# The diagonals, the first queries' weights, the value scaling and the turned heads of a decoder block, placed anew

## The chip, the cores and the metric

The kernel runs on one core of one Trainium2 chip. The metric is the device time of one execution in microseconds (us). The kernel before took 1434.86 us, the median of 3 runs (1434.17 to 1435.17).

## What is computed

One layer of a decoder block on x of 1024 positions by 1024 channels, in float32. The input is normalized by rows and projected; two branches work on the projection, differential attention with a distance bias and chunkwise retention; sigmoid gates merge them; a gated MLP with a short causal convolution follows. Cut to what matters:

```python
h = rms_norm(x, g_mix)                       # 1024 x 1024
q1, q2, k1, k2, va, qr, kr, vr, gr, gate_a, gate_r = split(h @ w_in)
# differential attention: 4 heads, keys of 64, values of 128 channels
s1 = q1 @ k1.T / 8 - slope * dist            # causal; s2 from q2, k2 likewise
a = (softmax(s1) - lam * softmax(s2)) @ va
a = rms(a) * g_diff_sub * (1 - lam_init)     # by head
r = rms(retention(qr, kr, vr)) * silu(gr)    # 4 heads, chunks of 128
merged = sigmoid(gate_a) * (a @ w_diff_proj) + sigmoid(gate_r) * (r @ w_ret_proj)
x = x + merged @ w_out
zg, zu = split(causal_dwconv(rms_norm(x, g_ffn) @ w_up))
x = x + (silu(zg) * zu) @ w_down
out = rms_norm(x, g_final)
```

## The kernel before, in words

**Precision.** Every large product is made of three TensorE products of rounded float32 parts. An operand is split into a part "hi" (a copy of rounded type, made by ACT) and a part "lo" (what the copy lacks, a subtraction on DVE or POOL); then hi x hi, hi x lo and lo x hi go into one PSUM bank. `split`, `product` and `gemm` (L206, with `weight` at L163 and L164 for the weights) do that.

**The first stretch.** It is written in plain order and laid out by a scheduler that puts each instruction on its engine as soon as its inputs are due. x comes in eight blocks of 128 channels. The values of heads 0 and 1 (`ps_va0`) and 2 and 3 (`ps_va1`) are multiplied from x times the gain `g_mix`, before the rows' norms are known: `u` holds the split parts of that product, in pool places "br", "c", "vo" and "s". The norms of the rows stand in `rst_x` (two tiles of 128 x 4, one for each half of the positions). `to_va` (L395) copies a bank of values into `va[h]` on ACT; later POOL multiplies each `va[h]` by `rst_x` in two halves (L433), eight products in all. `across` (L262, L263) spreads `rst_x` along a row: DVE makes four diagonal tiles, one TensorE product with ones turns them into `row_x`, a bank of 128 x 512, for each half. x is loaded again as it was, eight blocks of 512 KB into six places "s", and normalized (L418 to L420): DVE multiplies by gain and row, ACT makes the hi part `hT[0]`, and the lo part `hT[1]` is made by DVE for the first half of the positions (c = 0) and by POOL for the second (c = 1).

**The attention.** `queries_keys(h)` multiplies the queries and the keys of a head from hT: a bank `psq` or `psk` for each half of the positions, 24 products of 128 x 512 in each. Its weights come through the pools "wraw", "whi" and "wlo" of two places each; POOL makes their lo parts. Both banks of a product come from the two banks of PSUM tag "g". ACT and DVE empty them (L471 on, L478 to L481). For each block of 128 queries `attention` multiplies scores `pss` (banks "x"), which DVE adds to the distance table `dist_t` while it takes the minimum (L507), ACT exponentiates them (L512), DVE joins the two maps, TensorE transposes the result (`pat`, banks "b", L525), ACT empties that (L527), TensorE multiplies by the values (`po`, L530). `dist_t` is the one tile of pool tag "g" from then on; `ssum` holds that place before it. Its load is issued on POOL's queue (L438). The products for the queries and keys of the second and of the third head run between the blocks of the first head's attention.

**The steps.** From the fourth head on the order is written by hand. A step is 24 products of 128 x 512 or some 12 of them (24 for two halves); `step` notes its loads, sums, products and what follows them (`post`), and `issue` puts out the loads 9 steps ahead, sums 4, hi parts 3 and lo parts 2 steps ahead, then what stands in `pre` of the step, then its products, then its `post`. `at_step` appends to the `post` of a step; `n_gates` is the number of the first step of the attention's output projection (`ps_pa`). The last seven steps before it are parts of the gates' products, named (pair, part): (11,2), (10,4), (11,5), (11,6), (11,3), (11,7), (11,4). `turn_a(h)` (L787) transposes head h's attention output, eight 128 x 128 transposes into the two banks "b"; `finish_a(h)` empties these banks, first two ACT copies to the hi part (L803), then two DVE subtractions to the lo part (L805). Both stand in a post:

```python
at_step(n_gates - 7 + h, partial(turn_a, h))
at_step(n_gates - 6 + h, partial(finish_a, h))
```

so head h+1's transposes come behind the products of step n_gates - 6 + h, and head h's emptying behind those same products' own emptying.

## Time and profile before

| | |
|---|---|
| runs, us | 1434.86 median of 3 (1434.17 to 1435.17) |
| the profiled execution, us | 1434.84, of which its span 1433.0 |
| mean clock granted to TensorE | 0.984 |
| TensorE (PE) busy | 1368.6 us, 96%, 6472 instructions |
| VectorE (DVE) busy | 1068.0 us, 75%, 1699 instructions |
| ScalarE (ACT) busy | 703.4 us, 49%, 1318 instructions |
| GpSimd (POOL) busy | 154.3 us, 11%, 92 instructions |
| HBM traffic | 136.81 MB read, 49.55 MB written |

Busy time is the time in which an engine has an instruction at work, from one profiled execution. All durations quoted further on are of that execution; its 1434.84 us are the span and 1.84 us around it. [...]

### The profile page before, as it was taken

The page shows a single profiled execution, that of the slowest core. Times are in us where ns is not written, and L with a number is a line of the kernel's source. Part 1 is how long each engine was busy: PE and PEld are TensorE (multiplying, and loading weights), DVE is VectorE, ACT ScalarE, POOL GpSimd, SP SyncE. Part 2 cuts the span into 40 slices and gives each one's busy share as a digit, 9 for nine tenths or more (in the row PEclk, how much of TensorE's full clock was granted, in tenths as well). Part 3 has the DMA queues.
Part 4 walks back from the last instruction along what each step waited for, and adds up shares of the span by engine and source line. Part 5 has one row for each costly group of instructions (what it writes and reads, how often), then busy time and mean ns, then how long its engine had stood idle before and what let it go on. Part 6 is the DMA issues. An engine that isn't in the chain of part 4 may idle for free.

```text
span 1433.0 us, 18055 instructions
## 1 busy us (share of the span) xinstructions
PE 1368.6 (96%) x6472; PEld 1134.0 (79%) x6472; DVE 1068.0 (75%) x1699; ACT 703.4 (49%) x1318; POOL 154.3 (11%) x92
## 2 busy tenths in 40 slices
PE   7899899989999998999998989999999999999996
PEld 7887788878888886788776767888888888888885
DVE  6759765675655553467968989888988899897876
ACT  6544665564454434221445465455555556444452
POOL 6711001000000000000000012111111112200000
PEclk9999999999999999999989999999999999999997
DMA  7313101314334332635324134434433365943223
GB/s 250 125 45 121 56 16 45 137 70 143 137 125 136 108 110 81 251 138 180 153 100 148 59 113 159 133 122 136 139 126 125 125 228 195 331 165 103 94 90 118
DMA packets 81018, 187.55 MB, mean 131 GB/s; under 512 B 8320, under 2 KB 18944, under 8 KB 80928
## 3 DMA queue, kind: packets, MB, share of 16 engines
q1 hardware_dynamic: 80736, 185.74, 37.8%
q8 instruction: 51, 0.84, 0.2%
q0 software_dynamic: 192, 0.66, 0.1%
q14 instruction: 39, 0.32, 0.1%
HBM read 136.81 MB, written 49.55 MB: 130 GB/s over the span
## 4 chain that ended last, share of the span: by engine, by line
PE 42%; DVE 7%; ACT 1%; issue 1%; DVEq 0%; ACTq 0%
PE up L276 24%; PE wd L276 14%; PE wo L276 4%; DVE wf L285 1%; DVE f L285 1%; DVE x L1461 1%; DVE y L1381 1%; DVE ssum L228 1%; DVE x L1230 1%; DVE x L288 1%; DVE x L285 0%; ACT f L291 0%; DVE zg L288 0%; DVE raw_zg L285 0%; DVE wwo L285 0%
## 5 line engine op out<-in xcount | busy, mean ns | idle before, releaser
L276 PE MATMUL up<-f,wf 128*128 128x512 f32 x1848 | 424.8, 391 | 9.2 <-DVE wf L285 3.4
L276 PEld LDWEIGHTS up<-f,wf 128*128 128x128 f32 x1848 | 345.3, 188 | 88.1 <-DVE wf L285 6.4
L276 PE MATMUL wd<-awd,wwd 128*128 128x512 f32 (+1 forms) x960 | 212.2, 383 | 0.0
L276 PEld LDWEIGHTS wd<-awd,wwd 128*128 128x128 f32 x960 | 176.0, 189 | 35.4 <-issue 0.5
L285 POOL TENSOR_TENSOR t12g<-y 128x512 f32<-128x512 f32 x11 | 19.8, 1796 | 673.3 <-DVE y L1391 538.4
L276 PE MATMUL wo<-awo,wwo 128*128 128x512 f32 x336 | 83.2, 407 | 7.4 <-DVE awo L285 7.1
L276 PEld LDWEIGHTS wo<-awo,wwo 128*128 128x128 f32 x336 | 64.9, 196 | 24.8 <-DVE awo L285 10.1
L512 ACT ACTIVATE s<-s,row 128x512 f32<-128x512 f32 (+7 forms) x64 | 49.5, 773 | 26.7 <-DVE row L507 26.2
L1381 DVE SCALAR_TENSOR_TENSOR y<-zg,par,y 128x1022 f32<-128x1022 f32 (+1 forms) x44 | 58.6, 1333 | 2.9 <-ACT y L1378 2.9
L502 PE MATMUL pss<-k,q 128*128 128x512 f32 (+2 forms) x192 | 52.8, 371 | 5.6 <-DVE row L507 5.5
L288 DVE TENSOR_TENSOR zg<-zg,up 128x512 f32<-128x512 f32 x44 | 30.2, 685 | 37.0 <-PE up L276 34.6
L1381 DVE SCALAR_TENSOR_TENSOR y<-zu,par,y 128x1022 f32<-128x1022 f32 (+1 forms) x44 | 56.1, 1277 | 0.0
L291 ACT ACTIVATE zg<-up 128x512 f32<-128x512 f32 x44 | 26.1, 596 | 58.5 <-PE up L276 58.5
L285 DVE TENSOR_TENSOR awd<-act_in,awd 128x512 fp32r<-128x512 f32 x77 | 53.7, 697 | 0.0
L507 DVE CUSTOM_DVE_ANT_0 s<-pss,dist_t 128x512 f32<-128x512 f32 (+3 forms) x64 | 37.0, 587 | 21.1 <-PE pss L502 19.7
L291 ACT ACTIVATE awd<-act_in 128x512 fp32r<-128x512 f32 x77 | 47.5, 616 | 0.3 <-DVE wf L285 0.2
L276 PE MATMUL ps_pa<-a,wpa 128*128 128x512 f32 x192 | 46.0, 394 | 0.0
L206 PE MATMUL psq<-hT,hi_q 128*128 128x512 f32 x128 | 43.2, 415 | 2.5 <-ACT hi_q L163 1.7
L291 ACT ACTIVATE zu<-up 128x512 f32<-128x512 f32 x44 | 26.2, 596 | 39.2 <-PE up L276 39.1
L276 PE MATMUL ps_pr<-r,wpr 128*128 128x512 f32 x192 | 43.7, 389 | 0.0
L291 ACT ACTIVATE wwd<-wdv 128x512 fp32r<-128x512 f32 x33 | 20.9, 632 | 46.1 <-PE wd L276 37.1
L530 PEld LDWEIGHTS po<-va,at 128*128 128x128 f32 x288 | 38.1, 195 | 6.2 <-ACT at L527 4.1
(367 smaller groups left out, 2822.9 us busy)
## 6 DMA issues: line engine op xcount, KB each, us to landing
act_in<-act SPq DMA_DIRECT2D x77, 256.0 KB, 2.9
act<-y SPq DMA_DIRECT2D x55, 256.0 KB, 2.2
raw_zg<-in_wall SPq DMA_DIRECT2D x22, 512.0 KB, 3.4
raw_zu<-in_wall SPq DMA_DIRECT2D x22, 512.0 KB, 4.1
x<-in_x SPq DMA_DIRECT2D x15, 512.0 KB, 7.8
act<-t12g SPq DMA_DIRECT2D x22, 256.0 KB, 2.0
wdu<-in_wall SPq DMA_DIRECT2D x22, 256.0 KB, 4.8
wdv<-in_wall SPq DMA_DIRECT2D x22, 256.0 KB, 5.7
```

What stands on the lines that cost most here:

```text
L206: nc.tensor.matmul(ps, w, a, start=i == 0, stop=i == n - 1)
L228: engine.tensor_tensor(self.ssum, self.ssum, sq, op=ALU.add)
L276: nc.tensor.matmul(ps[:, cols], w[:, x * 512 + at : x * 512 + at + P], a[y][:, cols], start=start and i == 0, stop=stop and i == n - 1, sk ...
L285: engine.tensor_tensor(out, a, b, op=ALU.subtract)
L288: engine.tensor_tensor(out, a, b, op=ALU.add)
L291: nc.scalar.activation(out, a, AF.Copy)
L502: nc.tensor.matmul(ps[:, : max(n, 256)], qs[m][:, i * P : (i + 1) * P], k[:, c : c + max(n, 256)], start=e == 0, stop=e == 1,)
L507: nc.vector.tensor_tensor_reduce(s[:, c : c + n], ps[:, :n], dst_t[:, S - width + c : S - width + c + n], SLOPES[h], low_, op0=ALU.add, op ...
L512: nc.scalar.activation(s[:, :width], s[:, :width], AF.Exp, bias=low_, scale=-1.0, accum_out=z[:, m : m + 1])
L530: nc.tensor.matmul(po, at[:, k * P : (k + 1) * P], va[h][:, kb, :], start=kb == 0, stop=kb == i)
L1230: nc.vector.scalar_tensor_tensor(y, y, gain(1, at), row, op0=ALU.mult, op1=ALU.mult)
L1381: nc.vector.scalar_tensor_tensor(y[side][:, n:], z[:, : S - n], t[:, j : j + 1], y[side][:, n:], op0=ALU.mult, op1=ALU.add)
```

## The change

It has five parts.

1. `across`: the eight diagonal tiles `diag_x` are made by ACT (a copy scaled by a column of `rst_x`) instead of DVE.
2. The values of heads 2 and 3 are multiplied by `rst_x` where ACT empties their banks. POOL's four products for these two heads are gone; the four for heads 0 and 1 stand behind the first head's queries and keys in the program text.
3. x is loaded again by halves of its rows: eight pieces of 256 KB for the first 512 positions, then eight for the second, two to a place of pool "s". DVE makes the lo part for both halves.
4. The first head's query weights have places of their own: the hi part in a place "br" (`q_br`), the lo part in the place "g" that `ssum` leaves and `dist_t` takes (`q_g`). Their load and split stand ahead of the normalizing, and DVE makes their lo part and that of the first key weights. The first head's products go queries c = 0, keys c = 0, queries c = 1, keys c = 1, with banks of "g" and "x" in turn.
5. `finish_a(h)` stands in the `pre` of step n_gates - 6 + h, ahead of its products, instead of in its `post`.

```diff
--- before.py
+++ after.py
@@ -259,7 +259,7 @@
         n = r.shape[1]
         diag = t4("at", f"diag_{name}", shape=(P, 512))
         for i in range(n):
-            nc.vector.tensor_scalar(diag[:, i * P : (i + 1) * P], ident, r[:, i : i + 1], None, op0=ALU.mult)
+            nc.scalar.activation(diag[:, i * P : (i + 1) * P], ident, AF.Copy, scale=r[:, i : i + 1])
         nc.tensor.matmul(ps, ones, diag[:, : n * P], start=True, stop=True)
         return ps
 
@@ -390,9 +390,9 @@
             if k == 3:
                 nc.sync.dma_start(out=cst, in_=consts)
 
-        def to_va(st, p, ps):
+        def to_va(st, p, ps, scale=1.0):
             for h in range(2 * p, 2 * p + 2):
-                nc.scalar.activation(va[h][:, st, :], ps[:, h % 2 * DV : (h % 2 + 1) * DV], AF.Copy)
+                nc.scalar.activation(va[h][:, st, :], ps[:, h % 2 * DV : (h % 2 + 1) * DV], AF.Copy, scale=scale)
 
         for st in range(NST):
             to_va(st, 0, first_ps[st])
@@ -411,26 +411,18 @@
                     for k in range(KB)
                 ],
             )
-            to_va(st, 1, ps)
-
-        def normalize(src, h, k, cs, g, row, dst, helper):
-
-            nc.vector.scalar_tensor_tensor(h, src, gain(g, k), row, op0=ALU.mult, op1=ALU.mult)
-            nc.scalar.activation(dst[0][k][:, cs], h, AF.Copy)
-            helper.tensor_tensor(dst[1][k][:, cs], h, dst[0][k][:, cs].bitcast(F32), op=ALU.subtract)
-
-        for k in range(KB):
-            xt = t4("s", f"xn{k}")
-            nc.sync.dma_start(out=xt, in_=xT[k * P : (k + 1) * P, :])
-            for c in range(2):
-                cs = slice(c * 512, (c + 1) * 512)
-                normalize(xt[:, cs], xt[:, cs], k, cs, 0, rows[c], hT, (nc.vector, nc.gpsimd)[c])
-
-        for h in range(NH):
-            for c in range(2):
-                v = va[h][:, 4 * c : 4 * c + 4, :]
-                r = rst_x[c].rearrange("p (a b) -> p a b", b=1)
-                nc.gpsimd.tensor_tensor(v, v, r.broadcast_to([P, 4, DV]), op=ALU.mult)
+            to_va(st, 1, ps, rst_x[st // 4][:, st % 4 : st % 4 + 1])
+
+        w_q0 = weight(("q", 0), [t4(tag, f"q0_{tag}", F32R) for tag in ("br", "g")])
+        for c in range(2):
+            cs = slice(c * 512, (c + 1) * 512)
+            for k in range(KB):
+                if k % 2 == 0:
+                    pair = t4("s", f"xn{c}_{k}")
+                x = pair[:, k % 2 * 512 : (k % 2 + 1) * 512]
+                nc.sync.dma_start(out=x, in_=xT[k * P : (k + 1) * P, cs])
+                nc.vector.scalar_tensor_tensor(x, x, gain(0, k), rows[c], op0=ALU.mult, op1=ALU.mult)
+                split(x, hT[0][k][:, cs], hT[1][k][:, cs])
 
         lam_in = t4("at", "lam_in", shape=(P, 2, 2, HD))
         nc.gpsimd.dma_start(out=lam_in.rearrange("p a b d -> p (a b d)"), in_=lams)
@@ -480,8 +472,17 @@
                     for b in (low, top):
                         nc.vector.tensor_tensor(kl[b, cs], ps[a], kh[a, cs].bitcast(F32), op=ALU.subtract)
 
-            gemm(("q", h), "g", f"q{h}", queries, nc.gpsimd)
-            gemm(("k", h), "g", f"k{h}", keys, nc.gpsimd)
+            if h:
+                gemm(("q", h), "g", f"q{h}", queries, nc.gpsimd)
+                gemm(("k", h), "g", f"k{h}", keys, nc.gpsimd)
+                return qs, ks
+
+            ws = [w_q0, weight(("k", 0))]
+            for c in range(2):
+                for n, w, done in zip("qk", ws, (queries, keys)):
+                    ps = psum("gx", f"ps{n}{h}_{c}")
+                    channel_major(ps, w, of_h, KB, c)
+                    done(slice(c * 512, (c + 1) * 512), ps)
             return qs, ks
 
         def attention(h, qs, ks, blocks=(3, 7, 6, 5, 4, 2, 1, 0)):
@@ -705,6 +706,11 @@
                     pairs[i + e].add(p)
 
         qk = queries_keys(0)
+        for h in range(2):
+            for c in range(2):
+                v = va[h][:, 4 * c : 4 * c + 4, :]
+                r = rst_x[c].rearrange("p (a b) -> p a b", b=1)
+                nc.gpsimd.tensor_tensor(v, v, r.broadcast_to([P, 4, DV]), op=ALU.mult)
         for h in range(NH - 1):
             attention(h, *qk)
             qk = queries_keys(h + 1)
@@ -903,7 +909,7 @@
         for h in range(NH):
             at_step(18 + h, lambda h=h: scale_heads(oa[h], rstd_a[:, h * NST : (h + 1) * NST]))
             at_step(n_gates - 7 + h, partial(turn_a, h))
-            at_step(n_gates - 6 + h, partial(finish_a, h))
+            steps[n_gates - 6 + h].pre.append(partial(finish_a, h))
 
 
         MERGED = ("br",) * 5 + ("s", "s", "vo")
```

Three places of the order that results; a row is an engine's instruction with the line of the kernel that it stands in (line numbers behind 410 differ by a few between the two).

The first query weights on ACT, which makes their hi part, before (`hi_q_788` is that part of head 0, `raw_q_787` the load, `hT_7` the last block of hT, `va_94` and `va_95` the values of heads 2 and 3):

```order
L395 ACTIVATE va_94<-ps_va_6_640 128x128
L395 ACTIVATE va_95<-ps_va_6_640 128x128
L419 ACTIVATE hT_7_80<-xn_750 128x512
L163 ACTIVATE hi_q_788<-raw_q_787 128x1024
L395 ACTIVATE va_94<-ps_va_7_667 128x128
L395 ACTIVATE va_95<-ps_va_7_667 128x128
L163 ACTIVATE hi_k_852<-raw_k_851 128x1024
L471 ACTIVATE q_0_781<-psq_0_793 64x512
```

and with the change (`q_br` is that hi part):

```order
L253 ACTIVATE rst_x_437<-tiny_x_436,eps 128x4
L163 ACTIVATE q_br<-raw_q_696 128x1024
L262 ACTIVATE diag_x_453<-cst,rst_x_437 128x128 x4
L253 ACTIVATE rst_x_445<-tiny_x_444,eps 128x4
L262 ACTIVATE diag_x_460<-cst,rst_x_445 128x128 x4
L395 ACTIVATE va_94<-ps_va_0_478,rst_x_437 128x128
L395 ACTIVATE va_95<-ps_va_0_478,rst_x_437 128x128
```

The split of the first query weights stands behind the first `rst_x` now, ahead of all diagonals and of the whole normalizing; before, it was the last ACT work but one ahead of the first queries' emptying.

The third head's queries on PE, which run between the blocks of the first head's attention (`psq_0` and `psq_1` are their two halves, `pss_5_1_512` the second piece of the scores of query block 5's second map), before:

```order
L206 MATMUL psq_0_1727<-hT_7_88,hi_q_1722 128x512
L206 MATMUL psq_0_1727<-hT_7_80,lo_q_1723 128x512
L502 MATMUL pss_5_1_512_1069<-k_0_785,q_0_782 128x256
L502 MATMUL pss_5_1_512_1069<-k_0_786,q_0_782 128x256
L502 MATMUL pss_4_0_0_1101<-k_0_783,q_0_781 128x512
L502 MATMUL pss_4_0_0_1101<-k_0_784,q_0_781 128x512
L206 MATMUL psq_1_1756<-hT_0_73,hi_q_1722 128x512
L206 MATMUL psq_1_1756<-hT_0_81,hi_q_1722 128x512
```

and with the change, at the same place and at the place to which the score products went:

```order
L206 MATMUL psq_0_1731<-hT_7_88,hi_q_1726 128x512
L206 MATMUL psq_0_1731<-hT_7_80,lo_q_1727 128x512
L206 MATMUL psq_1_1760<-hT_0_73,hi_q_1726 128x512
L206 MATMUL psq_1_1760<-hT_0_81,hi_q_1726 128x512
L206 MATMUL psq_1_1760<-hT_0_73,lo_q_1727 128x512
L206 MATMUL psq_1_1760<-hT_1_74,hi_q_1726 128x512
```

```order
L206 MATMUL psq_1_1760<-hT_6_87,hi_q_1726 128x512
L503 MATMUL pss_5_1_512_1073<-k_0_791,q_0_788 128x256
L503 MATMUL pss_5_1_512_1073<-k_0_792,q_0_788 128x256
L206 MATMUL psq_1_1760<-hT_6_79,lo_q_1727 128x512
L503 MATMUL pss_4_0_0_1105<-k_0_789,q_0_787 128x512
L503 MATMUL pss_4_0_0_1105<-k_0_790,q_0_787 128x512
```

The scores `pss_5_1_512` and `pss_4_0_0` stood ahead of the products of `psq_1`; they stand behind 20 and 21 of its 24 now.

The turned heads on ACT (`pta_0` and `pta_1` are the two banks of turned blocks, `a_...` the hi part, `z_gt` a gate, `wgt` a weight's hi part), before:

```order
L619 ACTIVATE z_gt_4687<-pa_gt_4542 128x512
L619 ACTIVATE z_gt_4687<-z_gt_4687 128x512
L803 ACTIVATE a_4827<-pta_0_4798,gd 128x512
L803 ACTIVATE a_4827<-pta_1_4803,gd 128x512
L291 ACTIVATE wgt_7_4847<-raw_gt_4566 128x512
L291 ACTIVATE z_gt_4863<-pb_gt_4850 128x512
L803 ACTIVATE a_4865<-pta_0_4833,gd 128x512
```

and with the change:

```order
L809 ACTIVATE a_4815<-pta_0_4802,gd 128x512
L809 ACTIVATE a_4815<-pta_1_4807,gd 128x512
L620 ACTIVATE z_gt_4691<-pa_gt_4546 128x512
L620 ACTIVATE z_gt_4691<-z_gt_4691 128x512
L291 ACTIVATE wgt_7_4851<-raw_gt_4570 128x512
L809 ACTIVATE a_4854<-pta_0_4837,gd 128x512
L809 ACTIVATE a_4854<-pta_1_4842,gd 128x512
```

The two copies out of the turned banks stand ahead of the gate's emptying of the same step instead of behind it, and so do DVE's two subtractions on their engine.

## Rows read from the trace of the kernel before

**Rows 1.** Windows of three stretches; first line: the columns.

```profile
core 0: us, PE busy (x) PEld busy (x) DVE busy (x) ACT busy (x) POOL busy (x), PEclk, DMA share, GB/s
60.00:80.00 20.00, 16.18 (x77) 13.24 (x76) 7.39 (x9) 6.88 (x15) 11.80 (x8) 0.91 0.16 52
140.00:160.00 20.00, 16.33 (x89) 13.67 (x88) 17.29 (x48) 12.47 (x36) 1.41 (x1) 0.83 0.23 80
550.00:600.00 50.00, 42.54 (x185) 33.70 (x184) 17.05 (x27) 15.70 (x26) 0.00 (x0) 0.93 0.43 151
```

**Rows 2.** Timeline, PE and ACT, 62 to 69: start, us, engine, line, work [idle <-releaser].

```profile
62.97 0.28 PE L206 MATMUL ps_va<-hi_va,u 128*128 128x256 f32 x1
...
63.81 1.05 ACT L163 ACTIVATE hi_q<-raw_q 128x1024 fp32r<-128x1024 f32 x1
...
64.92 1.20 PE L206 MATMUL psq<-hT,hi_q 128*128 128x512 f32 x4 [1.68 <-ACT hi_q L163]
...
68.26 0.50 PE L206 MATMUL psq<-hT,lo_q 128*128 128x512 f32 x1 [2.15 <-POOL lo_q L164]
```

**Rows 3.** Timeline, PE, 81 to 91.

```profile
81.11 0.39 PE L206 MATMUL psk<-hT,lo_k 128*128 128x512 f32 x1
...
81.79 0.39 PE L206 MATMUL psk<-hT,lo_k 128*128 128x512 f32 x1
...
90.86 1.07 PE L502 MATMUL pss<-k,q 128*128 128x512 f32 x4
```

**Rows 4.** Timeline, first stretch: weights, norms, rows, normalizing; landing of raw_q.

```profile
35.49 0.33 SPq L196 DMA_DIRECT2D raw_q<-in_wall  x1
DMA to landing us min/median/max: 3.3/3.8/4.3
38.62 0.26 ACT L253 ACTIVATE rst_x<-tiny_x,eps 128x4 f32<-128x4 f32 x1
44.33 2.71 DVE L418 SCALAR_TENSOR_TENSOR xn<-xn,par,row_x 128x512 f32<-128x512 f32 x4
44.64 1.10 PE L263 MATMUL row_x<-diag_x,cst 128*128 128x512 f32 x2 [0.63 <-DVE diag_x L262]
```

**Rows 5.** Chain of waits: four ACT diagonals of a later stage.

```profile
778.67 1.29 ACT diag_f L1149 x4
```

**Rows 6.** Landing of dist_t (its tile's view).

```profile
DMA to landing us min/median/max: 3.8/3.8/3.8
```

**Rows 7.** Timeline, DVE and PE, first head's attention.

```profile
91.62 0.69 DVE L507 CUSTOM_DVE_ANT_0 s<-pss,dist_t 128x512 f32<-128x512 f32 x1 [0.72 <-issue]
129.17 1.40 DVE L481 TENSOR_TENSOR k<-psk,k 64x512 fp32r<-64x512 f32 x2
130.71 1.19 PE L206 MATMUL psq<-hT,hi_q 128*128 128x512 f32 x2 [0.79 <-DVE k L481]
133.52 0.48 DVE L507 CUSTOM_DVE_ANT_0 s<-pss,dist_t,row 128x256 f32<-128x256 f32 x1
146.08 0.54 DVE L507 CUSTOM_DVE_ANT_0 s<-pss,dist_t 128x384 f32<-128x384 f32 x1
```

**Rows 8.** Waits of PE: engine, work, line <- releaser: us in all, count, longest.

```profile
PE pta L787 <- DVE a L805: 6.7, 3, 2.6
```

**Rows 9.** Timeline, PE, 556 to 576.

```profile
556.67 1.77 PE L787 MATMUL pta<-cst,oa 128*128 128x128 f32 x8 [2.57 <-DVE a L805]
...
575.95 2.89 PE L276 MATMUL pa_gt<-ht,wgt 128*128 128x512 f32 x12
```

**Rows 10.** Window at the end of (10,4)'s products.

```profile
554.00:555.00 1.00, 0.10 (x1) 0.00 (x0) 0.00 (x0) 0.86 (x2) 0.00 (x0) 1.00 0.00 0
```

**Rows 11.** Transposes amid the first head's attention: timeline, PE, and their window.

```profile
117.09 1.03 PE L525 MATMUL pat<-cst,s 128*128 128x128 f32 x8
117.88 1.05 PE L502 MATMUL pss<-k,q 128*128 128x384 f32 x4
116.00:118.00 2.00, 2.00 (x15) 1.75 (x14) 1.97 (x3) 1.47 (x3) 0.00 (x0) 1.00 0.01 2
```

## The prediction

> **What bounds the kernel now.** The summary of engines comes first: TensorE is busy for 96% of the span, so time can only come from the 64 us in which it idles or from stretches at half clock. The slices of the span then show where: the granted clock is below full at the start, around 140 us, around 550 to 600 us and at the very end. The windows of those stretches show TensorE busy 16.18 of 20 us with the clock at 0.91 (60 to 80), 16.33 of 20 at 0.83 (140 to 160) and 42.54 of 50 at 0.93 (550 to 600) [rows 1]. The timeline of TensorE and its list of waits then name what each idle stretch waited for. Two of these the change touches: the first head's query products, which wait for the split of their weights [rows 2], and the transposes of the attention's output, which wait for the banks that DVE empties last [rows 8]. Between them lies the first head's attention, where DVE sets the pace (17.29 of 20 us busy there [rows 1]).
>
> **Part by part.** All is worked out against the profiled execution, 1434.84 us, which is 0.02 under the median shown.
>
> *A, the first stretch (parts 1 to 4).* The last value product ends at 62.97 + 0.28 = 63.25 [rows 2]; the first score product starts at 90.86 [rows 3]. Those 27.6 us hold 96 products of queries and keys. Three of them start within 81.79 − 81.11 = 0.68 us [rows 3], 0.2267 each, 21.8 for 96. The other 27.6 − 21.8 = 5.85 us are idle time of 1.68 and 2.15, behind ACT's hi part and POOL's lo part of the query weights [rows 2], and products at half clock behind them. With the weights split early both go. To that comes the 0.63 in which `row_x` waits for DVE's diagonals [rows 4]. **A gains 6.45 us**, if four things hold:
>
> - The weights must not hold up what stands behind them. ACT's split comes right behind the first `rst_x`, which ends at 38.62 + 0.26 = 38.88 [rows 4]. The load is issued at 35.49 before and lands 3.3 to 4.3 us later, so by 39.8 [rows 4]; if it is issued as early as now, the split, 1.05 us [rows 2], ends near 40.85.
> - ACT's diagonals: four took 1.29 us at a later stage [rows 5], so the first four end near 42.15. Before, DVE's first multiplication by `row_x` started at 44.33 [rows 4]; since some value products now stand ahead of `row_x` on TensorE, I take 44.6.
> - hT in time: eight multiplications on DVE take 0.68 each (2.71 for four [rows 4]), and eight lo parts of the same shape, taken as equal, another 5.4. The first half is done by about 44.6 + 10.9 = 55.5, long before the products begin, now at 63.25 − 0.63 = 62.6. The second half is loaded as the places of the first come free and takes another 10.9; with a us or two for the last loads it is done by about 68. It is wanted when the first halves of queries and keys, 48 products, are through: 62.6 + 10.9 = 73.5. POOL's second-half work, which moves to DVE, costs 8 x 0.68 = 5.4 us of DVE, inside that slack.
> - `dist_t` waits for the place of the query weights' lo part, whose last product now ends 72 products behind the start, at 62.6 + 16.3 = 78.9. Its landing takes 3.8 us [rows 6]; with somewhat under a us for POOL's issue it is there near 83. The first score product moves to 90.86 − 6.45 = 84.4, and DVE's first use of the table, at 91.62 before [rows 7], to about 85.1: 2 us to spare.
>
> The values' scaling (part 2) takes four products from POOL and gives ACT nothing new, only a scale on copies it makes anyway; POOL's four remaining ones stand behind the first queries and are done well before `po` needs them. I cost it at nothing; its cover is POOL's idleness after the first stretch.
>
> *The first head's attention.* From the first score product on, the instructions are the same, but TensorE's order is not. Counted from that product, the third head's second query half started at 130.71 − 90.86 = 39.85 us, behind DVE's emptying of the keys, 129.17 + 1.40 [rows 7]. The scores `pss_5_1_512` stood ahead of it and were drained at 133.52, 42.7 in [rows 7]. Now they stand behind 20 of its products. With TensorE released at about 39.3 in, 20 products take 4.5 us, and the first of them run at half clock after the idle time (some 1.8 us more); DVE drains them near 46.7, 4 us later. DVE has other work for about half of that. I take **2.1 us given back**. The bounds: with that order DVE could eat all of A (it is busy for nearly all of this stretch, and its instructions are not fewer), or the order could gain, up to the 20 − 16.33 = 3.67 us of idle time in the window at 140 [rows 1].
>
> *B, the turned heads (part 5).* Step (10,4)'s products end by 554.10 (TensorE is busy for 0.10 of the us from 554 [rows 10]), and step (11,7)'s start at 575.95 [rows 9]: 21.85 us. In them stand three heads' transposes, eight at 117.88 − 117.09 = 0.79 us [rows 11], 2.4 for 24, and 36 products at 0.2267, 8.2. So 10.6 us of work; 6.7 of the remaining 11.3 are the three waits for DVE [rows 8], the others are transposes and products at half clock after each of them: eight transposes take 1.77 us after the first wait [rows 9] and 1.03 amid other work [rows 11], while the clock granted up to that wait was 1.00 [rows 10]. With the emptying ahead of the step's own products, the two banks come free during them. At the tightest step ACT has a gate and a weight to work on ahead of its two copies, and by the durations of such operations now I estimate the first bank free about 3.3 us and the second 4.0 us after the transposes before it; TensorE's 12 products and the half of the next transposes bring it there at 3.7 and 4.1. That slack is little, so I take 0.8 off the full gain: **B gains 10.5 us**. The gate's emptying now stands behind two ACT copies and two DVE subtractions; a bank of the gates is wanted again only a step later. The bounds: 6.7 if only the waits go and the clock stays low, 11.3 if all goes.
>
> For the clock part of B one row decides. Between 116 and 118 TensorE did eight transposes and scores, and the clock granted was 1.00 [rows 11]. [...]
>
> Sum: 1434.84 − 6.45 + 2.1 − 10.5 = **1420.0 us**.
>
> **The rivals.**
>
> - *The attention gives nothing back.* DVE absorbs the later scores, or the new order gains. 1434.84 − 6.45 − 10.5 = 1417.9 down to 1414.2 with the 3.67. For it: the bound engine's work is the same, and a later score can be filled with other work. Against: DVE's tight order there, which leaves it little to do when one score is late.
> - *The attention eats A whole.* DVE's instructions set the end of that stretch, whose start then gains nothing: 1434.84 − 10.5 = 1424.3. For it: 17.29 of 20 us busy [rows 1]. Against: DVE too can start 6 us earlier, as it waits for the scores then (0.72 idle ahead of its first table use [rows 7]).
> - *Transposes keep the clock low.* Eight of them between two steps' products let the granted clock fall, as the idle time does now. Then only the 6.7 of waits go: 1434.84 − 6.45 + 2.1 − 6.7 = 1423.8. For it: the stretch has three such places close together. Against: the window at 116 [rows 11]. [...]
> - *The change does not do what it says at the turned heads*: the banks come free too late and the waits stay in part. With half of B: 1420.0 + 5.3 = 1425.3.
> - *Slower.* `dist_t` now stands behind the first queries' products instead of at 41 us. If its load is queued behind the halves of x and lands later than 85.1, DVE's first score waits, and with it all that DVE does up to the end of the first attention. Each us late is one us lost. To come out slower it has to eat all that the forecast gains, 1434.84 − 1420.0 = 14.8 us, so to land after 85.1 + 14.8 = 99.9, 21 us after its place is free, where it took 3.8 [rows 6]; at 103 the time would be 1438.
>
> **How the numbers follow.** What a measurement of this kernel can tell from no change is 0.2%, 2.9 us. Chances: the forecast, within 1417.9 to 1423, 0.50; nothing given back or a gain (1414 to 1417.9) 0.18; A eaten whole (1424.3) 0.16; transposes at low clock (1423.8) 0.05; turned heads still waiting (1425 to 1428) 0.05; several small mishaps that leave it within 0.2% of before 0.03; slower 0.03. All but the last two are faster by over 2.9 us: 0.94. The range runs from 1413.5 (all three terms at their best: 6.45 + 3.67 + 11.3 gives 1413.4) to 1426.0, which takes in the eaten A and leaves out only B's lower half with it (1434.84 − 6.7 = 1428.1).
>
> **What would show each step.** Right: no idle time of TensorE ahead of the first `psq`, the first score product at about 84.4, the first table use without a wait for a DMA; s for block 2's second map 57 us behind the first score product, where it was 146.08 − 90.86 = 55.2 [rows 7]; no wait of `pta` for `a`, granted clock 1.00 from the end of (10,4) on, and (11,7) starting 11.3 to 10.5 us sooner after it. Wrong: idle time of TensorE ahead of the keys' or the second half's queries (hT late), a wait of DVE for `dist_t`, `pta` still waiting on DVE or now on ACT, and a loss in the first head's attention beyond 2 us. If the time comes out under 1413 a stall that I did not look at went away with these.

## The result and the profile after

The change makes the kernel faster: 1419.46 us, median of 4 runs (1416.42 to 1423.54), against 1434.51 before, median of 4 runs (1431.19 to 1435.17). The ratio is 0.9893, interval 0.9864 to 0.9923. The forecast was 1420.0, range 1413.5 to 1426.0. The profiled execution took 1420.92 us, its span 1419.1, at a mean granted clock of 0.988 (a share of full speed). One execution of experiment 9, of 3514.85 us against some 1425 for the others of its kernel, is left out of that experiment's ratio and median.

The busy time by engine, first part of the page of after:

```profile
PE 1362.4 (96%) x6472; PEld 1131.8 (80%) x6472; DVE 1067.1 (75%) x1701; ACT 706.3 (50%) x1326; POOL 137.7 (10%) x78
```

TensorE has 6 us less of busy time with the same number of instructions: the mean clock rose from 0.984 to 0.988, so less of them ran at half clock. POOL lost 14 instructions (four products of values, eight lo parts of hT, two of the first weights), ACT gained the eight diagonals.

Windows of after, the stretches of [rows 1] and one more (columns as there):

```profile
60.00:80.00 20.00, 20.00 (x109) 17.33 (x108) 11.71 (x20) 9.31 (x18) 5.48 (x1) 1.00 0.25 85
140.00:160.00 20.00, 16.79 (x75) 14.27 (x76) 15.97 (x48) 11.31 (x34) 0.00 (x0) 0.74 0.17 69
550.00:600.00 50.00, 49.06 (x237) 40.21 (x235) 26.47 (x40) 16.48 (x27) 0.00 (x0) 1.00 0.63 225
552.00:566.00 14.00, 14.00 (x77) 11.86 (x76) 8.26 (x13) 8.71 (x16) 0.00 (x0) 1.00 0.35 131
```

The first stretch is full now and the third nearly so (49.06 of 50 us), both at full clock; the one in the first head's attention is no better, its clock even lower (0.74 for 0.83).

The first stretch on TensorE, timeline of after; it answers to [rows 2] and [rows 3]:

```profile
64.42 0.28 PE L206 MATMUL ps_va<-hi_va,u 128*128 128x256 f32 x1
64.54 0.63 PE L206 MATMUL psq<-hT,q_br 128*128 128x512 f32 x2
...
86.33 0.61 PE L503 MATMUL pss<-k,q 128*128 128x512 f32 x2
```

Both waits ahead of the queries are gone. From the first query product to the first score product it takes 86.33 − 64.54 = 21.79 us.

The distance table, timeline of POOL and landing from the table's own view, and its first use on DVE; they answer to [rows 6] and [rows 7]:

```profile
81.36 0.58 POOL L430 DMA_DIRECT2D dist_t<-in_dist  x1 [9.41 <-PE psq L206]
...
DMA to landing us min/median/max: 3.6/3.6/3.6
...
86.98 0.69 DVE L508 CUSTOM_DVE_ANT_0 s<-pss,dist_t 128x512 f32<-128x512 f32 x1 [1.50 <-PE pss L503]
```

The distance table is there by 81.36 + 0.58 + 3.6 = 85.5 at the latest, and DVE waits for the scores, not for it.

The turned heads, timeline of TensorE in after; it answers to [rows 8] to [rows 10]:

```profile
551.34 1.03 PE L793 MATMUL pta<-cst,oa 128*128 128x128 f32 x8
...
554.98 1.03 PE L793 MATMUL pta<-cst,oa 128*128 128x128 f32 x8
...
562.24 1.03 PE L793 MATMUL pta<-cst,oa 128*128 128x128 f32 x8
563.03 2.98 PE L276 MATMUL pb_gt<-hT,wgt 128*128 128x512 f32 x12
565.85 2.88 PE L276 MATMUL pa_gt<-ht,wgt 128*128 128x512 f32 x12
```

No row has a wait, and each eight transposes take 1.03 us, where they took 1.77 behind the first wait before. Each row of eight is one head. From the end of (10,4) at 554.98 to the start of (11,7) at 565.85 it is 10.87 us, for 21.85 before.

**Where the time went, by stretches.** The table is worked out from the start times of TensorE's products in each profile; a column is the time from one of these products to the next: the first value product, the last product of the norms (`tiny_x`), the first query product, the first score product, the third head's first key product, the fourth head's first key product, the first transpose of the turned heads, the first product of (11,7), the last product. "Before 2" is a second profile of the kernel before.

```
                start  to psq  to pss  to k3  to k4   to pta  to (11,7)  rest    sum
before          31.90   26.05   25.94  64.67  45.23   349.54   25.64   847.60  1416.58
before 2        34.07   26.04   26.94  64.75  45.19   350.38   25.30   843.31  1415.99
after           34.17   23.35   21.79  69.01  45.21   350.79   14.51   843.83  1402.66
first_only      32.48   23.35   21.79  68.79  45.21   350.49   25.42   843.83  1411.35
turned_only     34.09   25.90   26.93  64.71  45.21   351.78   14.51   845.89  1409.03
turned_again    32.55   26.05   26.70  64.63  45.21   352.20   14.51   847.35  1409.21
diag_dve        33.70   24.58   21.79  67.41  45.23   349.36   14.51   846.94  1403.52
weights_wraw    34.01   23.35   23.48  70.09  45.28   349.79   14.51   846.92  1407.45
lo_pieces       32.76   23.35   21.79  65.87  45.89   350.69   14.51   844.71  1399.56
att_first       32.91   23.35   18.84  68.34  46.12   350.99   14.51   843.28  1398.35
lo_att          31.91   23.35   18.84  65.21  46.14   348.63   14.51   845.30  1393.89
sums_later      32.64   23.35   21.79  54.31  59.64   350.08   14.51   843.30  1399.63
sums_split      33.58   23.35   21.79  60.05  56.81   349.28   14.51   845.20  1404.56
sums_last_lo    34.58   23.35   21.79  54.32  47.02   364.68   14.51   842.89  1403.14
```

Three stretches move with the change: the first by 26.05 + 25.94 − 23.35 − 21.79 = 6.85 us gained, the first head's attention by 69.01 − 64.67 = 4.34 lost, the turned heads by 25.64 − 14.51 = 11.13 gained. That is 13.64 of the 13.92 between the two sums. Against the second profile of before, whose "to pss" is 1.0 us longer, the first gain is 7.84 us and the last 10.79. The other stretches are within the scatter: "start", "to pta" and "rest" differ by 2.2, 0.8 and 4.3 us between the two profiles of the same kernel before. One place where they differ is the stretch at 715 us, windows of before and then of the second profile of before:

```profile
715.00:765.00 50.00, 45.01 (x176) 35.13 (x176) 37.93 (x63) 23.27 (x44) 0.00 (x0) 0.90 0.33 114
...
715.00:765.00 50.00, 44.77 (x186) 34.74 (x186) 40.13 (x67) 24.42 (x46) 0.00 (x0) 0.97 0.33 116
```

The program and TensorE's order are the same, the granted clock is not; the two windows do not hold quite the same products (176 and 186).

### The profile page after: what moved, and what is told of

It is laid out like the page before. It is cut to its first block, busy times and chain, and to the rows that moved or that the text cites. A ratio compares the mean times of both kernels' runs of the same rounds, so it can differ in the third digit from the quotient of the medians.

```text
span 1419.1 us, 18038 instructions
## 1 busy us (share of the span) xinstructions
PE 1362.4 (96%) x6472; PEld 1131.8 (80%) x6472; DVE 1067.1 (75%) x1701; ACT 706.3 (50%) x1326; POOL 137.7 (10%) x78
## 4 chain that ended last, share of the span: by engine, by line
PE 42%; DVE 8%; ACT 1%; issue 1%; DVEq 0%; ACTq 0%
PE up L276 24%; PE wd L276 14%; PE wo L276 3%; DVE wf L285 1%; DVE f L285 1%; DVE x L1467 1%; DVE y L1387 1%; DVE ssum L228 1%; DVE x L288 1%; DVE x L1236 0%; DVE x L285 0%; ACT f L291 0%; DVE zg L288 0%; DVE raw_zg L285 0%; DVE wwo L285 0%
## 5 line engine op out<-in xcount | busy, mean ns | idle before, releaser
L531 PE MATMUL po<-va,at 128*128 128x128 f32 x288 | 41.1, 288 | 2.1 <-ACT at L528 2.1
```

What stands on the lines that cost most here:

```text
L531: nc.tensor.matmul(po, at[:, k * P : (k + 1) * P], va[h][:, kb, :], start=kb == 0, stop=kb == i)
```

## Experiments

**1. The turned heads alone (turned_only).** The kernel before with part 5:

```diff
-            at_step(n_gates - 6 + h, partial(finish_a, h))
+            steps[n_gates - 6 + h].pre.append(partial(finish_a, h))
```

> The kernel before with part 5 alone. From the end of (10,4) to the start of (11,7), 21.85 us before and 11.2 with the whole change: all theories say 11 to 12 here. Theory 1 (the turned heads carry all of the gain, and what the whole change gains behind 600 us is their doing too): the time falls by 13 to 15 us, to about 1420. Theory 2 (the turned heads are worth their 10.5 and the rest comes from elsewhere, from the first parts or by chance of the clock): it falls by 10 to 11, to about 1424.

Measured: ratio 0.9947 (0.9933 to 0.9962), median 1426.23, 7.2 us under the 1433.42 of before in these runs. The stretch itself gives what it gives in the whole change, 14.51 us; (10,4)'s end to (11,7)'s start, timeline of TensorE:

```profile
559.04 1.03 PE L787 MATMUL pta<-cst,oa 128*128 128x128 f32 x8
...
569.91 2.88 PE L276 MATMUL pa_gt<-ht,wgt 128*128 128x512 f32 x12
```

569.91 − 559.04 = 10.87. Neither theory's total came: the fall, 5.4 to 9.6 us by the interval, is smaller than both say. Theory 1 falls: nothing behind 600 us is shorter by part 5.

**2. The first parts alone (first_only).** The whole change without that part:

```diff
-            steps[n_gates - 6 + h].pre.append(partial(finish_a, h))
+            at_step(n_gates - 6 + h, partial(finish_a, h))
```

> The whole change without part 5 (the turned heads are emptied behind the step, as before). Theory 1 (the first head's attention eats what the first stretch gains): first score product near 86.3 instead of 90.9, the emptying of the third head's second query half at 151.5 instead of 152.3 as with the whole change, and the time at most 1 us under before. Theory 2 (my forecast's terms: 6.45 gained, 2.1 given back): 4.3 us under before, about 1430.

Measured: ratio 0.9975 (0.9963 to 0.9987), 1429.80, 3.6 us under before. The waits of TensorE show the turned heads as before:

```profile
PE pta L793 <- DVE a L811: 6.7, 3, 2.6
```

By the stretches, 6.85 gained and 68.79 − 64.67 = 4.1 lost, 2.7 net (3.8 against the second profile of before). Theory 1 falls. Theory 2's 4.3 lies within the interval of the median, 1.9 to 5.3 us; by the stretches the attention eats more than the 2.1 forecast, but not all.

**3. POOL's lo parts in four pieces (lo_pieces).** The whole change, and in `split`:

```diff
+        if engine is nc.gpsimd:
+            for i in range(0, 1024, 256):
+                cs = slice(i, i + 256)
+                engine.tensor_tensor(lo[:, cs], src[:, cs], hi[:, cs].bitcast(F32), op=ALU.subtract)
+            return
```

> The whole change with each of POOL's lo parts of query and key weights made in four pieces of 256 columns instead of one of 1024; TensorE's order is the same. Theory 1 (in the first head's attention DVE's subtractions stand behind POOL's long lo parts: two took 2.78 and 3.36 us with the change where such a one takes 0.69 and 1.22, some 4.2 us lost, where the kernel before lost 2.2): those two come down to under 1.4 and 1.9 us, the emptying of the third head's second query half comes 1 to 3 us sooner than 151.5, and the time falls by about as much. Theory 2 (TensorE's order, with the scores behind the queries' products, sets the end): DVE's operations may get shorter, but that emptying stays within 0.5 us of 151.5 and the time with it.

Measured: 1417.16 (1416.12 to 1417.78), ratio 0.9887 (0.9874 to 0.99). What it acts on, timeline of POOL and DVE, first before:

```profile
120.85 2.40 POOL L164 TENSOR_TENSOR lo_k<-raw_k,hi_k 128x1024 fp32r<-128x1024 f32 x1 [11.17 <-ACT hi_k L163]
...
122.01 1.79 DVE L285 TENSOR_TENSOR ta<-tb,ta 128x512 f32<-128x512 f32 x1
...
139.03 2.38 POOL L164 TENSOR_TENSOR lo_q<-raw_q,hi_q 128x1024 fp32r<-128x1024 f32 x1 [15.79 <-ACT hi_q L163]
...
140.17 2.32 DVE L288 TENSOR_TENSOR ta<-hT,hT 128x1024 f32<-128x1024 f32 x1
```

then after the change:

```profile
118.11 2.88 POOL L164 TENSOR_TENSOR lo_k<-raw_k,hi_k 128x1024 fp32r<-128x1024 f32 x1 [12.60 <-ACT hi_k L163]
...
118.03 0.69 DVE L285 TENSOR_TENSOR ta<-tb,ta 128x512 f32<-128x512 f32 x1
118.76 2.78 DVE L285 TENSOR_TENSOR tb<-tb,ta 128x512 f32<-128x512 f32 x1
...
135.73 2.37 POOL L164 TENSOR_TENSOR lo_q<-raw_q,hi_q 128x1024 fp32r<-128x1024 f32 x1 [14.75 <-ACT hi_q L163]
...
135.82 3.36 DVE L288 TENSOR_TENSOR ta<-hT,hT 128x1024 f32<-128x1024 f32 x1
```

and with the pieces:

```profile
116.55 3.74 POOL L167 TENSOR_TENSOR lo_k<-raw_k,hi_k 128x256 fp32r<-128x256 f32 x4 [12.26 <-ACT hi_k L163]
...
117.18 1.11 DVE L290 TENSOR_TENSOR tb<-tb,ta 128x512 f32<-128x512 f32 x1
...
133.01 5.01 POOL L167 TENSOR_TENSOR lo_q<-raw_q,hi_q 128x256 fp32r<-128x256 f32 x4 [12.72 <-ACT hi_q L163]
...
133.10 1.73 DVE L293 TENSOR_TENSOR ta<-hT,hT 128x1024 f32<-128x1024 f32 x1
```

In these rows a DVE operation on two operands in SBUF that starts while POOL's is running ends only behind it: at 122.01 one of 0.69 us waits for POOL's end at 123.25, at 135.82 one of 1.22 for 138.10. Before, DVE came half-way into POOL's operation and lost 1.1 us each; with the change it comes early in it and loses 2.1 each. With the pieces these two lose 0.4 and 0.5, but three more operations lose about 0.5 each:

```profile
119.62 1.23 DVE L290 TENSOR_TENSOR tb<-tb 128x512 f32<-128x512 f32 x1
...
134.75 1.48 DVE L523 SCALAR_TENSOR_TENSOR s<-s,row,s 128x768 f32<-128x768 f32 x1
...
137.37 1.74 DVE L293 TENSOR_TENSOR tb<-hT,hT 128x1024 f32<-128x1024 f32 x1
```

So DVE's loss falls from 4.2 to 2.5 us, not to nothing. The emptying of the second query half came at 147.13 us for 151.47, 2.7 sooner when the 1.64 us are taken off by which this execution's first query product came earlier (62.90 for 64.54). The stretch is 69.01 − 65.87 = 3.1 us shorter, with the order of TensorE and of DVE unchanged. So theory 1 holds for the emptying; the median, 2.3 us under that of the change, is within the scatter of the two.

Not all of the 3.1 us is the waiting itself. Two waits of TensorE for DVE become shorter, waits from 60 to 166 us, of after and then of this kernel:

```profile
PE psq L206 <- DVE k L473: 3.2, 1, 3.2
PE pat L526 <- DVE s L518: 2.0, 1, 2.0
PE pss L503 <- DVE row L508: 1.0, 2, 0.6
...
PE psq L211 <- DVE k L478: 2.1, 1, 2.1
PE pat L531 <- DVE s L523: 0.8, 1, 0.8
PE pss L508 <- DVE row L513: 1.9, 3, 0.8
```

That is 2.3 us, and a third wait, of the scores for `row`, grows by 0.9. Behind the second stand twelve value products, timeline of TensorE in after, in diag_dve (experiment 8) and in this kernel:

```profile
141.57 2.93 PE L531 MATMUL po<-va,at 128*128 128x128 f32 x12 [0.18 <-ACT at L528]
...
141.71 1.60 PE L531 MATMUL po<-va,at 128*128 128x128 f32 x12 [0.17 <-ACT at L528]
...
137.69 1.61 PE L536 MATMUL po<-va,at 128*128 128x128 f32 x12 [0.18 <-ACT at L533]
```

They ran at half clock in after (in first_only too, 2.93 us) and at full clock in the other two. diag_dve has the two waits and DVE's long operations as in after, yet its stretch took 67.41 us. So up to 1.6 of the 3.1 us can be the clock, which fell in two profiles of three with the same waits; against diag_dve the pieces give 67.41 − 65.87 = 1.5 us.

**4. The attention ahead in priority (att_first).**

```diff
-            attention(h, *qk)
+            with tc.high_priority():
+                attention(h, *qk)
```

> The whole change with the attention's instructions ahead in the scheduler's priority of the queries and keys of the next head; in TensorE's order the scores of block 5's second map and of block 4 then stand ahead of the third head's second query half again. Theory 1 (waits behind POOL): the emptying of that second query half changes by less than 1 us from 151.5 unless the waits behind POOL change as well. Theory 2 (the order): from the first score product to that emptying it takes some 61.5 us, as in the kernel before, instead of 65.1, and the time falls by 2 to 4 us.

Measured: 1416.92 (1416.48 to 1417.19), ratio 0.9886 (0.9873 to 0.9899). Theory 2 as it was put fell: from the first score product to that emptying it is 148.72 − 82.47 = 66.3 us. Theory 1 had said less than 1 us from 151.5, and fell too: the emptying came 2.75 us sooner, 0.9 of them by an earlier first query product. But the first score products themselves went ahead of the last key products, 18.84 us behind the first query product instead of 21.79, so the experiment is less clean than meant. From the first query product to the third head's keys it takes 18.84 + 68.34 = 87.18 us, for 21.79 + 69.01 = 90.80 with the change: 3.6 less, though two waits behind POOL are still there (one operation of 0.69 us took 2.89, one of 1.22 took 2.69). The second head's stretch is 0.9 longer. The order costs time too, but this run does not separate the scores at the third head's queries from those at the start.

**5. Both (lo_att).**

> The whole change with both of the last two edits: POOL's lo parts in four pieces, and the attention ahead in priority. Theory 1 (two separate losses in the first head's attention, the waits behind POOL and the order of TensorE): the gains add, 2.4 and 2.8 us from first product to the attention's second head, and the time is near 1414.5. Theory 2 (one loss, DVE's pace, which either edit relieves): no more than 1 us under the better of the two, 1416 to 1417.

Measured: 1413.08 (1412.5 to 1414.28), ratio 0.9852 (0.9827 to 0.9878). From the first query product to the third head's keys 18.84 + 65.21 = 84.05, 6.75 less than with the change; the two alone give 3.14 and 3.62, together 6.76. The gains add, so these are two separate losses, and theory 1 holds: theory 2 said at most 1 us under the better of the two, and the median is 3.8 under. That the sum fits to 0.01 us is luck, with 1.6 us of scatter in this stretch. This is the fastest kernel of the study.

**6. DVE's load (sums_later).** The sums of quarters moved behind the second head's attention:

```diff
-            if h == 0:
+            if h == 1:
                 h_sums()
```

> The whole change with the sums of the normalized input's quarters (some 21 us of DVE work, four times two of 1.22 and four of 0.69 us) made behind the second head's attention instead of the first's. Theory 1 (DVE's load sets the end of the first head's attention): TensorE's idle time and half clock there, some 13 us from 120 to 160 with the change, go for the most part, and the time is 1408 to 1414 if the later stretches have room on DVE. Theory 2 (the order of TensorE and the banks set it): that stretch gains under 2 us, and the time is at 1418 or above.

Measured: 1419.64, ratio 0.9899 (0.9877 to 0.9921). Windows of after, and then of this kernel:

```profile
100.00:160.00 60.00, 51.75 (x251) 43.28 (x250) 52.18 (x108) 28.99 (x67) 8.23 (x3) 0.89 0.26 97
160.00:200.00 40.00, 38.89 (x230) 33.67 (x229) 28.33 (x80) 26.51 (x63) 5.28 (x2) 1.00 0.09 27
...
100.00:160.00 60.00, 59.66 (x327) 50.66 (x327) 41.30 (x106) 37.90 (x86) 10.37 (x4) 1.00 0.11 31
160.00:200.00 40.00, 30.66 (x148) 24.43 (x147) 38.19 (x87) 18.29 (x47) 2.59 (x1) 0.84 0.29 114
```

With the sums' 21 us of DVE work gone from it the first head's stretch takes 54.31 us instead of 69.01, and TensorE is busy for 59.66 of 60 us there. So the sums, and with them DVE's load, do set the end of that stretch. But the second head's stretch takes 59.64 instead of 45.21: 14.7 gained, 14.4 given back.

**7. Half the sums in each (sums_split), and all behind the third head (sums_last_lo, with POOL's pieces).** `h_sums` was given the blocks to make, two behind the first head and two behind the second; in the other kernel all four stand at `h == 2`, and `split` is that of experiment 3.

```diff
-        def h_sums():
+        def h_sums(some):
...
-            if h == 0:
-                h_sums()
+            if h < 2:
+                h_sums(range(2 * h, 2 * h + 2))
```

> The whole change with the sums made half behind the first head's attention and half behind the second's, some 10 us of DVE each. Theory 1 (DVE's load sets the end of either stretch, and all 21 us in one of them are too many for it): TensorE runs nearly without idle time in both, the first head's stretch takes 55 to 60 us instead of 69 and the second's 93 to 97, and the time is 1406 to 1411. Theory 2 (the loss only moves and splits): each of the two is longer than TensorE's work by some 6 us, and the time is 1416 to 1420, as with all sums in the one or the other.

> The whole change with POOL's lo parts in four pieces and with all of the sums made behind the third head's attention, where from 200 to 250 us DVE is busy for 28 of 50 us and TensorE for all 50. Theory 1 (DVE sets the pace only in the first two heads' attention, and has room for 21 us behind them): the first head's stretch takes 55 us and the second's 93 to 95, the third's grows by less than 5, and the time is 1404 to 1410. Theory 2 (the sums cost some 12 to 16 us wherever they stand, as in the second head's attention): the third head's stretch grows by as much and the time is 1417 to 1421.

Measured: 1421.79, ratio 0.9918 (0.9897 to 0.9938), and 1423.76, ratio 0.9941 (0.9922 to 0.9959). Theory 1 fell both times; the times lie a little above theory 2's too. Halves: 9.0 us gained in the first head's stretch, 11.6 lost in the second's. At the end: 14.7 gained in the first, and "to pta" is 364.68, where the other profiles have 348.6 to 352.2. All of the sums cost TensorE 14.7 us in the first head's stretch (11.6 with POOL's pieces), 14.4 in the second's and 12.5 to 16.1 in the third's; the halves cost 5.7 and 11.6. The mean busy share of 28 of 50 us, from which I expected room behind the third head, did not show it.

**8. The weights' early places (weights_wraw) and the diagonals (diag_dve).**

```diff
-        w_q0 = weight(("q", 0), [t4(tag, f"q0_{tag}", F32R) for tag in ("br", "g")])
+        w_q0 = weight(("q", 0))
```

> The whole change without its own places for the first query weights: they come through the places that all weights share, and DVE splits them. Theory 1 (the early place is what takes the 1.68 and 2.15 us of waiting away): TensorE waits ahead of the first queries again, 2 us or more, and the first score product is 3 to 6 us later after the last value product than with the change (21.9 us). Theory 2 (DVE in POOL's stead and the halves are enough): no wait, 21.8 us from first query product to first score product.

```diff
-            nc.scalar.activation(diag[:, i * P : (i + 1) * P], ident, AF.Copy, scale=r[:, i : i + 1])
+            nc.vector.tensor_scalar(diag[:, i * P : (i + 1) * P], ident, r[:, i : i + 1], None, op0=ALU.mult)
```

> The whole change with the diagonals made by DVE again. Theory 1 (my term of 0.63 us): the product with the first diagonals waits 0.6 us again, or DVE's first half of the normalizing starts later, and everything behind is 0.6 us later. Theory 2 (with the change TensorE gets to that product later, behind more value products, so DVE's diagonals are ready by then): no wait and no difference of more than 0.3 us up to the first query product.

Measured: 1423.66, ratio 0.9917 (0.9885 to 0.9949), and 1420.20, ratio 0.9897 (0.9867 to 0.9928). TensorE's waits, timeline of weights_wraw and then of diag_dve:

```profile
66.40 1.21 PE L206 MATMUL psk<-hT,hi_k 128*128 128x512 f32 x4 [0.78 <-ACT hi_k L163]
...
67.90 0.50 PE L206 MATMUL psq<-hT,lo_q 128*128 128x512 f32 x1 [0.29 <-DVE lo_q L164]
...
47.68 1.10 PE L263 MATMUL row_x<-diag_x,cst 128*128 128x512 f32 x2 [1.00 <-DVE diag_x L262]
```

Without the early places the stretch to the first score is 1.7 us longer (23.48), under what theory 1 asked and over theory 2: the early places are worth 1.7 of the 6.85 us. The rest lies with the diagonals and with DVE in POOL's stead, the halves and the values' scaling, which were not run one by one. With DVE's diagonals the wait is back at the second half's `row_x`, and the stretch to the first query is 24.58 − 23.35 = 1.23 us longer: theory 1's mechanism at twice its size. The median does not tell it from the change; in the profiled execution the first head's stretch was 1.6 us shorter, by the clock shown in experiment 3.

**9. The scatter (before_again, turned_again).**

> The kernel before, unchanged, profiled once more, to see how its stretches differ from one execution to the next. Theory 1 (start and clock differ by chance): from TensorE's first product to the first query product it takes 58 to 60 us, where the first profile had 57.95 and the same program with the turned heads alone changed had 60.00; the stretches from 425 to 540 us and the turned heads agree within 0.3 us.

> The kernel before with part 5 alone, timed and profiled once more, since its first median lay 7.2 us under before where its profile shows 11 us less at the turned heads. Theory 1 (the executions scatter by their start and by the clock in other stretches): the turned heads take 13.1 to 13.2 us again and the median lies 8 to 12 us under before. Theory 2 (part 5 loses some 4 us elsewhere): the median is 6 to 8 us under before again, and a stretch behind 600 us is longer than in every profile without part 5.

Measured: before_again took 1434.36 us in its one run; it is "before 2" in the table. From the first product to the first query product it took 34.07 + 26.04 = 60.11 us, just over the 58 to 60 expected, and the turned heads 25.30 for 25.64. turned_again: ratio 0.9944 (0.9925 to 0.9964), the same as the first time, with 14.51 us at the turned heads again. The median is 1424.39, 8.3 us under before, and 8.0 by the ratio: at the edge between theory 1's 8 to 12 and theory 2's 6 to 8. So the total does not decide. Theory 2's stretch falls, since none behind 600 us is longer than every one without part 5 (its "rest" of 847.35 is under the 847.60 of before). Theory 1's scatter can be seen ahead of the turned heads. TensorE's order is the same in before and in both profiles of part 5 alone, and no engine's order differs ahead of 550 us; yet the clock differs near 290 us, windows of before and, 3 us on, of turned_only:

```profile
290.00:300.00 10.00, 8.27 (x52) 6.44 (x51) 8.09 (x25) 7.39 (x19) 0.00 (x0) 1.00 0.04 15
...
293.00:303.00 10.00, 8.27 (x45) 6.97 (x44) 7.04 (x22) 6.12 (x14) 0.00 (x0) 0.83 0.06 24
```

The second profile of part 5 has 0.83 there too, the second of before 1.00.

## Why the prediction was right, step by step

**A, the first stretch: right.** Forecast 6.45 (its terms, 5.85 and 0.63, give 6.48), measured 6.85, or 7.84 against the second profile of before. The 96 products took 21.79 us for the 21.8 worked out. The diagonals were worth more than the 0.63 of the row (1.23 in diag_dve). hT was in time: DVE's last subtraction for it ended near 69.7, where I had 68, and nothing waited for it. The distance table had 1.5 us to spare for the 2 forecast. The first score product came at 86.33 and not at 84.4 because this execution's start was 34.17 − 31.90 = 2.3 us longer; the kernel before has that too in its second profile.

**The first head's attention: the direction right, the size too small.** Forecast 2.1 us given back, measured 4.3 (2.7 in diag_dve, with the same waits of 3.2 and 2.0 us). The late scores came as worked out: they were drained 133.15 − 86.33 = 46.8 us behind the first score product, forecast 46.7. The 20 products ahead of them ran from 126.46 to 132.72, 6.26 us, for the 4.5 + 1.8 worked out; at 0.2267 each they take 4.53, and the granted clock was 0.50 from 128.4 to 130. Timeline of after, DVE:

```profile
133.15 0.48 DVE L508 CUSTOM_DVE_ANT_0 s<-pss,dist_t,row 128x256 f32<-128x256 f32 x1 [1.45 <-PE pss L503]
...
145.11 0.56 DVE L508 CUSTOM_DVE_ANT_0 s<-pss,dist_t 128x384 f32<-128x384 f32 x1 [0.22 <-PE pss L503]
```

Block 2's second map came 145.11 − 86.33 = 58.8 us behind, forecast 57. The step that failed is "DVE has other work for about half of that": I took DVE's durations as fixed, and the half was a guess that no row gave. Two of its operations stood behind POOL's lo parts and took 2.78 + 3.36 us, 4.2 more than alone; before, the same two kinds lost 2.2, and a third, at 108.78, another 0.8. So the missing term is 1.2 us of DVE's time over the whole stretch, 2.0 at these two places. lo_pieces, which cuts DVE's loss to 2.5 us at an unchanged order, gives 3.1 back against the profile of the change and 1.5 against diag_dve. The rows of experiment 3 show the blocking: the operation of 1.22 us that started at 135.82 ended 1.08 us behind POOL's end at 138.10; what blocks it in the chip no run shows. I had treated POOL's lo parts as work beside DVE's. The rest of the miss, up to 1.6 us, is the clock at which the value products of experiment 3 ran; why it fell here and in first_only and not in diag_dve stays open. With the pieces the stretch is still 65.87 − 64.67 = 1.2 us longer than before.

**B, the turned heads: right.** Forecast 10.5, measured 21.85 − 10.87 = 11.0 (first_only and after differ by 10.9 over the table's stretch), near the upper bound of 11.3: the tight slack held at all three steps, and the 0.8 that I took off was not needed in full. The clock part came as the row had it: 24 transposes stand in the window from 552 to 566, and the granted clock is 1.00; the lower bound of 6.7, at a clock that stays low, is not what came. "Half clock after each of them" was right for two of the three waits only: before, the clock was at 0.50 behind the first and the third, and at 1.00 behind the second, windows of before:

```profile
558.00:559.00 1.00, 1.00 (x5) 0.90 (x4) 0.00 (x0) 0.00 (x0) 0.00 (x0) 0.50 0.00 0
...
565.00:566.00 1.00, 1.00 (x7) 0.88 (x7) 0.60 (x2) 0.00 (x0) 0.00 (x0) 1.00 0.00 0
...
572.00:573.00 1.00, 1.00 (x5) 0.80 (x4) 0.00 (x0) 0.68 (x1) 0.00 (x0) 0.50 0.00 0
```

**The sum.** 6.45 − 2.1 + 10.5 was 14.85; the three measured terms give 13.64. The attention took 2.2 us more than forecast, and A and B gave 1.0 more together, so that errors partly offset each other. That the median hit the forecast within 0.6 us is partly chance: scatter of some us between executions of one kernel lies over it.

**The rivals.** The attention ate 4.3 of 6.85 us, half-way between the forecast and the rival in which it eats all. The turned heads did not wait, the transposes did not keep the clock low, the distance table did not hold up DVE. In weighing the second rival I took the 0.72 us ahead of DVE's first table use for a wait for the scores; that row of before says "issue", which names no wait. With the change the row names the scores (1.50).

**What stays open.** The parts alone give 0.53% (0.56% the second time) and 0.25%, the whole 1.07%: together 11 to 12 us of its 15. The interval of the whole, 0.77 to 1.36%, just takes that sum in. The turned heads show their 11.1 us in both profiles of part 5 alone, but both also show a longer "to pta" (351.78 and 352.20 for 349.54 and 350.38) and a "rest" above that of the second profile of before. The longer "to pta" is not the doing of part 5: it lies ahead of all that the part moves, and experiment 9 shows the lower clock in it. For the "rest", and for the clock falling there both times, no cause was found.

## What to carry to other kernels

Time saved ahead of a stretch that another engine paces is kept only as far as that engine's chain allows (here 6.85 − 4.34 = 2.5 of 6.85 us), so follow its chain through the new order with the durations that it will have there, not those that it had: an operation's row can contain a wait, as the 3.36 us of one of 1.22 did here. Where long operations of POOL (2.37 us and more here) stand beside DVE's operations on two operands in SBUF, try cutting them into pieces: here that took 1.7 of DVE's 4.2 us of waiting away, though more operations wait a little. And where a bank is emptied behind a step and wanted right after it, moving the emptying ahead of the step's own products can pay twice, as it did here: 6.7 us of waits, and 11.0 − 6.7 = 4.3 more, most of them in transposes and products that no longer run at half clock behind two of the three waits. And one profile of a stretch does not tell 1.6 us from the scatter; take two of each kernel.

## What the runs showed of the hardware

A DVE operation of 1.22 us took 3.36 us when it started 0.09 us behind POOL's subtraction, and no idle time or wait stands in its row: the wait is inside its duration. One with an operand in a PSUM bank did not wait: `s<-pss,dist_t` at 104.01 of after took 0.69 us, its usual time, inside POOL's subtraction from 102.52 to 105.51. Cut in four, POOL's operation took 5.01 us instead of 2.37 (lo_pieces), and DVE's three operations beside it 1.73, 1.48 and 1.74 us. The same twelve value products, behind the same six transposes and a wait of 2.0 us, took 2.93 us in one execution and 1.60 in another (after and diag_dve); the granted clock from 142 to 144 us was 0.50 in the one and 1.00 in the other.
